# First block with the bias turned earlier and 512-column products; last block with another product order, prior sums on GpSimd, a seed that takes its prior, and outputs in pieces

## The chip, the core and the metric

The kernel runs on one core of one Trainium2 chip. The metric is the time of one execution in microseconds on the device. Three runs of the kernel before took 848.92, 849.00 and 849.01 us; the median is 849.0 us.

## What is computed

x has 16 x 512 = 8192 rows of 768 columns, w1 is 768 x 3072, w2 is 3072 x 768, all in float32:

```python
def reference(x, w1, b1, w2):
    y = np.matmul(x, w1) + b1
    y = np.maximum(y, 0)
    return np.matmul(y, w2).astype(np.float32)
```

## The kernel before

**Blocks.** The 8192 rows are cut into 8 blocks of 1024 rows, and the 3072 hidden columns into two chunks. This gives 16 iterations (`NIT`): eight blocks for the first chunk, then eight for the second. In each one the first matrix product makes a piece y of the hidden layer (1024 rows by 1536 columns, in float16), and the second multiplies it by the matching 1536 rows of w2. What the first chunk gives is stored to the output; what the second chunk gives is added to it in DRAM, by stores on GpSimd's queue that accumulate. The last iteration (`final`) is an exception: seven of its eight output tiles (`LAST_DIRECT`) are not accumulated in DRAM. What the first chunk left there, the *prior*, is loaded into the tile x by SP's queue (line 1174), added on the core, and the finished tile is stored by SP's queue.

**Fewer products.** Both products are done by a bilinear scheme, as Strassen's is one: sums and differences of blocks of x, of w1, of y and of w2 are formed first (`X_SUMS`, `W1_SUMS`, `Y_SUMS`, `W2_SUMS`; on DVE, lines 828, 844, 1046, 862), and then 20 block products for each half of the hidden chunk take the place of 24, and 26 in the second matrix product take the place of 32. A product of the second kind is 6 matmuls of 128 x 128 by 384 columns (line 1199): two row tiles, j = 0 and 1, of three each. The products are gathered in *chains*: a chain keeps one pair of PSUM banks, and between its products it hands over what it has so far by operations (`SECOND_OPS`, line 1210 on ACT, line 1216 on DVE): a "sum" is kept in SBUF for another chain, a "seed" is written into the PSUM banks in which another chain starts, and an "out" finishes an output tile. `SECOND_ORDER` and, in the last iteration, `LAST_ORDER` say in which order the 26 products run.

**The first block** has no such sums: its products are plain (`add_plain`, line 983), because the sums of w1 are not there yet. A plain product makes 128 hidden columns (strip, j) for 512 rows (half m of the block). It runs in two parts of 256 rows (`parts` = 2, twelve matmuls) or at once (`parts` = 1, six matmuls of 512 columns). The x of this block is turned on PE (`add_transpose_first`, line 925): row tiles s = 0 to 3 of the first half in float32, loaded by the queues of SP and ACT in turn (line 711), then four of the second half in float16, loaded by GpSimd's queue. Each turn is two PSUM banks, copied to x by DVE and ACT (lines 933 and 931). The bias (`add_bias`) is loaded by ACT's queue (line 679), turned on PE (line 945), and made into small tables by DVE (lines 948 to 963). ACT takes each plain product out of PSUM with bias and relu (line 992).

**Order.** Nothing is scheduled on the chip. `Graph` plans the whole program when it is built: each piece of work is a task with an engine, a cost in ns, and what it reads and writes; `Graph.run` places tasks on five engines by these costs and due times, with PE's tasks kept in the order in which they were added; then the instructions are emitted in the order of planned starts, and each engine runs its own in that order, waiting on semaphores. So a changed cost or an added task can reorder work on DVE, ACT, GpSimd and SP near it.

**The end.** In the last iteration an "out" on DVE adds the prior to what is in PSUM. If another chain's sum belongs to it as well, that is added to the prior first (`prior_task`, line 1260, on DVE at a planned cost of 955 ns, or on GpSimd at 1850 if the operation is listed in `LAST_POOL`, which is empty before). `LAST_FOLD` = (5,) adds the prior of operation 5 into PSUM ahead of its chain's last product (`fold`, line 1277). The last "out", operation 1 (output tile 3, after product 20), is taken out in two halves by DVE (`half`), stored by the queues of ACT and SP (`store_half`, line 1245).

**The guard.** ACT also sums squares of the inputs (lines 767, 876, 890); a flag says at the end whether they were in the range for which float16 does, and a general path stands behind a branch that this data does not take.

Of the kernel before, what the change touches and what calls it, by code (L numbers as in the profile page):

```python
# [124 lines left out]
    24, 5, 20)  # L125
LAST_ORDER = (13, 15, 4, 17, 10, 8, 12, 18, 3, 0, 1, 14, 2, 19, 21, 11, 25, 23, 7, 16, 5, 6, 22,
    9, 24, 20)
LAST_FOLD = (5,)
LAST_DIRECT = (0, 1, 2, 3, 4, 5, 7)
LAST_POOL = ()  # L130

# [455 lines left out]
class Fast:  # L587
# [120 lines left out]
    def prologue(self):  # L708
        nc = self.nc
        for s in range(4):  # L710
            (nc.sync, nc.scalar)[s % 2].dma_start(out=self.s[:, s],
                                                  in_=self.xf[s * P:(s + 1) * P, :])
# [12 lines left out]
        for _ in range(8):  # L725
            nc.tensor.matmul(self.ps[:, 7, 0:P], lhsT=self.ones, rhs=self.ones, start=True,
                             stop=True)

    def presets(self):
        g = self.g  # L730
# [447 lines left out]
    def add_second(self, it):  # L1178
        c = it // self.NSB
        nc = self.nc  # L1180
        final = it == self.NIT - 1
# [10 lines left out]
        def pair(reg):  # L1192
            a = reg.at[0]
            return self.ps[:, a:a + 2, 0:NH]

        def product(p, ch, start):
            for j, h in ((j, h) for j in range(2) for h in range(3)):
                m0 = h * QM + j * P
# [37 lines left out]

        def half(t, j, dest):
            ch, a, _, _, _, to, _ = SECOND_OPS[t]
            out = self.s[:, dest.at[0], 0:NH]
            combine(nc.scalar if t in folds and j == 0 else nc.vector, out, pair(bank[ch])[:, j],  # L1240
                    a, None if t in folds else self.prior(to)[:, j], 1)

        def store_half(to, j, dest):
            s = self.s[:, dest.at[0], 0:NH]
            (nc.scalar, nc.sync)[j].dma_start(out=self.rows_of(it, to)[:, j], in_=s)

# [35 lines left out]
        where = {p: ch for ch, chain in enumerate(SECOND_CHAINS) for k, p in chain if k == "m"}  # L1282
        folds = set()
        for kind, n in steps:
            if kind == "m":
# [40 lines left out]
            else:  # L1326
# [4 lines left out]
                else:  # L1331
                    dest = bank[to] = Reg("ps", 2, seeded=1, leaves=1)
            if what == "out" and final and n == last:
                for j in range(2):
                    dest = Reg("s")
                    e = "ACT" if n in folds and j == 0 else "DVE"
                    self.g.add(e, 500, lambda t=n, j=j, dest=dest: half(t, j, dest),
                               reads=reads, writes=[dest])
                    self.g.add(("ACT", "SP")[j], 100, lambda to=to, j=j, dest=dest: store_half(to, j, dest),
                               reads=[dest], writes=[("half", j)], lat=3.5, dma=0.6)  # L1340
                continue
# [5 lines left out]
            if what == "out":  # L1347
# [3 lines left out]
                           reads=[dest], writes=[("out", self.block(it), to)],  # L1351
                           lat=3.5 if direct else 9.0, dma=1.2 if plain else 2.45)

# [191 lines left out]
```

## Time and profile before

| | |
|---|---|
| median of three runs (848.92 to 849.01) | 849.0 us |
| the profiled execution: span from its first to its last instruction | 847.4 us |
| PE busy | 839.4 us (99%) |
| DVE busy | 737.9 us (87%) |
| ACT busy | 569.4 us (67%) |
| GpSimd (POOL) busy | 164.1 us (19%) |
| granted clock of PE, mean | 0.999 |

The profiled execution has no time beside its span; the runs' median is 1.6 us above it.

A row of a timeline has the start, the length, the engine, the line, the operation, its tile written and read, its shape, the number of instructions merged in the row, and in brackets how long the engine sat idle ahead of it and what ended that. PEld is PE's weight load, which overlaps its products; a "q" behind an engine's name is its queue of DMA issues. PE's products overlap each other: the length of one (326 ns for 384 columns) is longer than the distance to the next.

### The profile page before, as it was taken

To read this page: it belongs to the slowest core of one execution; us is meant where nothing else is said; L and a number is where in the kernel's file an instruction comes from. 1 tells how busy PE (TensorE), PEld (TensorE's weight loads), DVE (VectorE), ACT (ScalarE), POOL (GpSimd) and SP (SyncE) were. 2 spreads that over 40 slices of the span, in tenths; PEclk is the share of its full clock that TensorE was granted. 3 is DMA by queue.
4 is the path that set the end of the run, shared out by engine and by line. 5 is a ranking of instruction groups with operands and counts; after the bars stand their busy time and mean duration, and the time that the engine had idled before them with its cause. 6 is when DMAs were issued, how large, how long until landed. Compare 5 with 4: busy or idle time off the path is not lost. (4 is left out here: it accounts for less than half of the span.)

```text
span 847.4 us, 16784 instructions
## 1 busy us (share of the span) xinstructions
PE 839.4 (99%) x6381; PEld 625.5 (74%) x6381; DVE 737.9 (87%) x1231; ACT 569.4 (67%) x1203; POOL 164.1 (19%) x179
## 2 busy tenths in 40 slices
PE   8999999999999999999999999999999999999997
PEld 7558778686786867768687686877868678686874
DVE  5898987969889697998999979798896979979788
ACT  5866876778677695756858558766757666456463
POOL 5210011102111010010030503224041230501300
PEclk9999999999999999999999999999999999999999
DMA  9996497978988678594793977979789797985836
GB/s 213 202 180 176 81 233 105 163 183 133 222 113 148 169 126 192 95 223 150 224 187 65 192 123 124 187 106 178 125 128 150 116 173 113 147 134 75 146 117 169
DMA packets 170967, 128.93 MB, mean 152 GB/s; under 512 B 93804, under 2 KB 169348, under 8 KB 170884
## 3 DMA queue, kind: packets, MB, share of 16 engines
q0 software_dynamic: 56560, 68.82, 53.1%
q1 hardware_dynamic: 113856, 58.02, 28.3%
q8 instruction: 50, 0.82, 0.4%
q10 hardware_dynamic: 468, 1.00, 0.3%
q14 instruction: 33, 0.27, 0.1%
HBM read 73.54 MB, written 69.21 MB: 168 GB/s over the span
## 5 line engine op out<-in xcount | busy, mean ns | idle before, releaser
L1199 PE MATMUL ps<-v,y 128*128 128x384 f16 x2496 | 408.4, 326 | 0.0
L1073 PE MATMUL ps<-x,v 128*128 128x256 f16 x3600 | 395.7, 273 | 0.0
L1073 PEld LDWEIGHTS <-v 128*128 128x128 f16 x3600 | 352.2, 98 | 42.4 <-issue 0.2
L1199 PEld LDWEIGHTS <-y 128*128 128x128 f16 x2496 | 244.2, 98 | 160.0 <-issue 0.2
L1210 ACT ACTIVATE s<-ps 128x384 f32<-128x384 f32 (+1 forms) x244 | 153.0, 646 | 121.3 <-PE ps L1199 120.2
L1046 DVE TENSOR_TENSOR y<-y 128x768 f16<-128x768 f16 (+1 forms) x384 | 219.4, 619 | 2.6
L1116 DVE CUSTOM_DVE_ANT_0 y<-ps,s 128x512 f16<-128x512 f32 x240 | 156.0, 686 | 54.4 <-ACT s L1113 41.4
L1252 POOL DMA_DIRECT2D out_dram<-s x78 | 93.9, 1470 | 145.4 <-ACT s L1210 97.0
L1113 ACT ACTIVATE s<-ps,bt 128x256 f32<-128x256 f32 x180 | 75.3, 470 | 62.5 <-PE ps L1073 56.7
L828 DVE TENSOR_TENSOR x<-x 128x768 f16<-128x768 f16 (+1 forms) x210 | 113.7, 579 | 1.3
L1113 ACT ACTIVATE y<-ps,bt 128x256 f16<-128x256 f32 x180 | 69.5, 486 | 10.8 <-PE ps L1073 10.8
L1210 ACT ACTIVATE ps<-ps 128x384 f32<-128x384 f32 (+1 forms) x144 | 67.9, 509 | 8.1 <-PE ps L1199 6.6
L1216 DVE TENSOR_TENSOR s<-ps,s 128x768 f32<-128x768 f32 x74 | 70.5, 953 | 1.2 <-issue 0.3
L706 POOL DMA_DIRECT2D xn<-in_x_dram x30 | 25.9, 863 | 214.0 <-DMA x<-xn 99.5
L1216 DVE TENSOR_TENSOR s<-s,ps 128x768 f32<-128x768 f32 x60 | 57.1, 951 | 2.2 <-DVE s L1216 0.5
L767 ACT ACTIVATE junk<-xn 128x768 f16<-128x768 f16 x64 | 54.0, 843 | 0.3
L1255 POOL DMA_DIRECT2D out_dram<-s x15 | 17.7, 1181 | 169.5 <-ACT s L1210 157.7
L1113 ACT ACTIVATE ps<-ps,bt 128x256 f32<-128x256 f32 x60 | 26.7, 445 | 32.4 <-PE ps L1073 31.4
L1109 ACT ACTIVATE ps<-ps 128x512 f32<-128x512 f32 x60 | 35.3, 588 | 4.1 <-DVE y L1116 3.5
L1124 DVE TENSOR_TENSOR s<-s,ps 128x512 f32<-128x512 f32 x30 | 20.6, 688 | 17.7 <-PE ps L1073 17.7
L983 PE MATMUL ps<-x,v 128*128 128x256 f16 (+1 forms) x216 | 32.0, 308 | 0.7 <-DVE x L933 0.7
L1119 DVE SCALAR_TENSOR_TENSOR s<-ps,bt,s 128x256 f32<-128x256 f32 x60 | 26.1, 477 | 4.4 <-PE ps L1073 4.4
(60 smaller groups left out, 304.8 us busy)
## 6 DMA issues: line engine op xcount, KB each, us to landing
out_dram<-s POOLq DMA_DIRECT2D x93, 384.0 KB, 8.8
out_dram<-s SPq DMA_DIRECT2D x70, 384.0 KB, 6.6
xn<-in_x_dram POOLq DMA_DIRECT2D x28, 768.0 KB, 9.7
x<-out_dram SPq DMA_DIRECT2D x7, 384.0 KB, 3.5
v<-in_w_dram POOLq DMA_DIRECT2D x6, 384.0 KB, 10.6
v<-in_w_dram POOLq DMA_DIRECT2D x12, 192.0 KB, 9.1
w1d<-in_w_dram POOLq DMA_DIRECT2D x6, 384.0 KB, 6.5
w2d<-in_w_dram POOLq DMA_DIRECT2D x12, 192.0 KB, 4.9
```

The source lines that it names most:

```text
L767: self.nc.scalar.activation(out=self.junk, in_=self.xn[:, s, :], func=ACTF.Square, accum_out=self.stat[:, self.stat_at["x"] + i:][:, 0:1])
L828: self.nc.vector.tensor_tensor(out=self.two(x, out), in0=self.two(x, in0), in1=self.two(x, in1), op=ALU.add if sign > 0 else ALU.subtract)
L983: nc.tensor.matmul(self.ps[:, ps.at[0], cols], lhsT=self.v1[:, gi, 2 * h + k2, k, j * P:(j + 1) * P], rhs=rhs, start=(k2 == 0 and k == 0), ...
L1046: self.nc.vector.tensor_tensor(out=self.two(self.y, out), in0=self.two(self.y, in0), in1=self.two(self.y, in1), op=ALU.add if sign > 0 els ...
L1073: nc.tensor.matmul(self.ps[:, at, j * self.QM:(j + 1) * self.QM], lhsT=self.v1[:, gi, self.w1s[c][gi][FIRST_V[p]], k, j * P:(j + 1) * P], ...
L1109: nc.scalar.activation(out=out, in_=ps, scale=float(a), func=func if kind == "out" else ACTF.Copy)
L1113: nc.scalar.activation(out=out[:, j], in_=ps[:, j], func=func, scale=float(a), bias=beta(j))
L1116: nc.vector._custom_dve(TENSOR_ADD_SAT, out=out, in0=ps, in1=s, s0=F_MAX, s1=0.0)
L1199: nc.tensor.matmul(self.ps[:, bank[ch].at[j], 0:NH], lhsT=self.y[:, ys[SECOND_U[p]], m0:m0 + P], rhs=self.v2[:, slot[SECOND_V[p]], h, :], ...
L1210: nc.scalar.activation(out=out, in_=ps, func=ACTF.Copy, scale=float(a))
L1216: engine.tensor_tensor(out=out, in0=in0, in1=in1, op=ALU.add if a == b else ALU.subtract)
L1252: nc.gpsimd.dma_start(out=rows, in_=out, accum_op=ALU.add)
```

## The change

Four things at the start. The bias is loaded between ACT's two loads of x and is turned on PE between the turns of row tiles 1 and 2 (before: between the two parts of the first product). Nine of the twelve plain products of strips 0 to 2 run at once with 512 columns; the first one of the first half and the first two of the second half stay in two parts. Row tiles 0 and 1 of the second half are turned ahead of a whole product (before: between its parts), and after row tiles 2 and 3 the product of strip 0, j = 1 runs between the two parts of that of j = 0. ACT takes all plain products of strips 0 to 2 out of PSUM in one operation. In the last iteration the order of products becomes ..., 23, 25, 7, 16, 5, 6, 9, 22, 20, 24, so operation 0 (output tile 2, after product 24) is the last. Nothing is folded. Operation 10, which writes the seed of product 24's bank, is done by DVE in two halves, and takes the prior of output tile 2 with it (`LAST_TAKE`), so the bank holds the finished sum after product 24. That product is added in two halves, each with its own wait. Operation 0 then only copies: 384 columns of j = 0 on ACT, stored by SP; 192 columns of j = 1 on DVE, stored by SP; the other 192 on ACT, stored by ACT (`LAST_PARTS`). Operation 1 (output tile 3) goes out in two halves on DVE, both stored by SP (`LAST_HALVES`). The sums of priors for operations 1, 3, 4 and 5 move to GpSimd (`LAST_POOL`).

```diff
+LAST_ORDER = (13, 15, 4, 17, 10, 8, 12, 18, 3, 0, 1, 14, 2, 19, 21, 11, 23, 25, 7, 16, 5, 6, 9,
+    22, 20, 24)
+LAST_FOLD = ()
+LAST_TAKE = {10: 0}
+LAST_HALVES = (1,)
+LAST_PARTS = ((0, 0, 384, "ACT", "SP"), (1, 0, 192, "DVE", "SP"), (1, 192, 384, "ACT", "ACT"))
 LAST_DIRECT = (0, 1, 2, 3, 4, 5, 7)
-LAST_POOL = ()
+LAST_POOL = (1, 3, 4, 5)
...
                                                   in_=self.xf[s * P:(s + 1) * P, :])
-        self.load_bias()
+            if s == 1:
+                self.load_bias()
...
-        g.preset("b1_rows", 5.0)
+        g.preset("b1_rows", 6.0)
...
         for s in range(4):
             self.add_transpose_first(0, s)
+            if s == 1:
+                self.add_bias()
         plain = self.add_plain
+
+        def turns(*tiles):
+            for s in tiles:
+                self.add_transpose_first(1, s)
         for strip in range(3):
             for j in range(2):
-                between = None
-                if strip == 0 and j == 0:
-                    between = self.add_bias
-                elif strip == 2 and j == 1:
-                    between = lambda: [self.add_transpose_first(1, s) for s in (0, 1)]
-                plain(strip, j, 0, 2, 2 if strip == 1 else 1, between)
-        plain(0, 0, 1, 2, 1, lambda: [self.add_transpose_first(1, s) for s in (2, 3)])
-        plain(0, 1, 1, 2, 1)
+                if strip == 2 and j == 1:
+                    turns(0, 1)
+                plain(strip, j, 0, 2 if strip == 0 and j == 0 else 1, 1)
+        plain(0, 0, 1, 2, 1, lambda: [turns(2, 3), plain(0, 1, 1, 2, 1)])
         for strip in (1, 2):
             for j in range(2):
-                plain(strip, j, 1, 2, 2 if strip == 1 else 1)
+                plain(strip, j, 1, 1, 1)
...
+        def part(t, j, cols, dest, e):
+            ch, a = SECOND_OPS[t][:2]
+            combine(nc.scalar if e == "ACT" else nc.vector, self.s[:, dest.at[0], cols],
+                    pair(bank[ch])[:, j, cols], a, None, None)
+
+        def store_part(to, j, cols, dest, e):
+            (nc.scalar if e == "ACT" else nc.sync).dma_start(
+                out=self.rows_of(it, to)[:, j, cols], in_=self.s[:, dest.at[0], cols])
...
+                if final and t == last and SECOND_CHAINS[ch][-2] == ("m", n):
+                    for j in range(2):
+                        self.g.add("PE", 488, lambda p=n, ch=ch, start=start, j=j:
+                                   product(p, ch, start, (j,)),
+                                   reads=self.y_keys(u) + [("w2", w, h) for h in range(3)] +
+                                   ([] if start else [bank[ch]]) +
+                                   ([("taken", t, j)] if t in taken_by else []),
+                                   writes=[("last", j)] + ([] if t in taken_by else [bank[ch]]))
+                    continue
...
+                for j, c0, c1, e, q in LAST_PARTS:
+                    dest = Reg("s")
+                    cols = slice(c0, c1)
+                    self.g.add(e, 100 + 1.05 * (c1 - c0),
+                               lambda t=n, j=j, cols=cols, dest=dest, e=e:
+                               part(t, j, cols, dest, e),
+                               reads=[("last", j)] + (reads if j else []), writes=[dest])
+                    self.g.add(q, 100, lambda to=to, j=j, cols=cols, dest=dest, q=q:
+                               store_part(to, j, cols, dest, q),
+                               reads=[dest], writes=[("part", j, c0)], lat=3.5, dma=0.545 * (c1 - c0) / 384)
+                continue
+            taken = LAST_TAKE.get(n) if final else None
+            if taken is not None:
+                assert engine == "ACT" and what == "seed" and SECOND_OPS[taken][1] == 1
+                folds.add(taken)
+                prior_task(taken)
+                of = SECOND_OPS[taken][5]
                 for j in range(2):
+                    self.g.add("DVE", 548, lambda ch=ch, a=a, of=of, dest=dest, j=j: combine(
+                        nc.vector, pair(dest)[:, j], pair(bank[ch])[:, j], a,
+                        self.prior(of)[:, j], 1),
+                        reads=reads + self.prior_keys(of) + ([dest] if j else []),
+                        writes=[("taken", taken, j)] + ([] if j else [dest]))
+                continue
...
```

More of the change, by code (lines that the diff above doesn't have):

```diff
@@ L125 @@
     24, 5, 20)
-LAST_ORDER = (13, 15, 4, 17, 10, 8, 12, 18, 3, 0, 1, 14, 2, 19, 21, 11, 25, 23, 7, 16, 5, 6, 22,
-    9, 24, 20)
-LAST_FOLD = (5,)
+LAST_ORDER = (13, 15, 4, 17, 10, 8, 12, 18, 3, 0, 1, 14, 2, 19, 21, 11, 23, 25, 7, 16, 5, 6, 9,
[4 more added lines that the diff above has]
+LAST_PARTS = ((0, 0, 384, "ACT", "SP"), (1, 0, 192, "DVE", "SP"), (1, 192, 384, "ACT", "ACT"))
 LAST_DIRECT = (0, 1, 2, 3, 4, 5, 7)
-LAST_POOL = ()
+LAST_POOL = (1, 3, 4, 5)
 X_FUSE = (3,)
@@ L1194, in pair, with product @@
             return self.ps[:, a:a + 2, 0:NH]
-        def product(p, ch, start):
-            for j, h in ((j, h) for j in range(2) for h in range(3)):
+        def product(p, ch, start, rows=(0, 1)):
+            for j, h in ((j, h) for j in rows for h in range(3)):
                 m0 = h * QM + j * P
@@ L1235, in operation @@
                         None if alone else sum_of(kept[u]), b)
[L1237 to L1245, printed above, removed]
+        def part(t, j, cols, dest, e):
[5 more added lines that the diff above has]
+                out=self.rows_of(it, to)[:, j, cols], in_=self.s[:, dest.at[0], cols])
         def store(to, reg, plain):
@@ L1283, in add_second @@
         folds = set()
+        taken_by = set(LAST_TAKE.values()) if final else ()
         for kind, n in steps:
@@ L1333, in add_second @@
             if what == "out" and final and n == last:
+                assert n in folds
+                for j, c0, c1, e, q in LAST_PARTS:
[8 more added lines that the diff above has]
+                               reads=[dest], writes=[("part", j, c0)], lat=3.5, dma=0.545 * (c1 - c0) / 384)
@@ new lines, in add_second @@
+                continue
[5 more added lines that the diff above has]
+                of = SECOND_OPS[taken][5]
+                for j in range(2):
+                    self.g.add("DVE", 548, lambda ch=ch, a=a, of=of, dest=dest, j=j: combine(
[4 more added lines that the diff above has]
+                continue
@@ L1334, in add_second @@
+            if what == "out" and direct and n in LAST_HALVES:
+                assert n not in folds
                 for j in range(2):
                     dest = Reg("s")
[L1336 to L1340, printed above, removed]
+                    self.g.add("DVE", 548, lambda j=j, to=to, ch=ch, a=a, dest=dest: combine(
+                        nc.vector, self.s[:, dest.at[0], 0:NH], pair(bank[ch])[:, j], a,
+                        self.prior(to)[:, j], 1), reads=reads, writes=[dest])
+                    self.g.add("SP", 100, lambda to=to, j=j, dest=dest: store_part(
+                        to, j, slice(0, NH), dest, "SP"),
+                        reads=[dest], writes=[("half", to, j)], lat=3.5, dma=0.545)
@@ L1351, in add_second @@
                            reads=[dest], writes=[("out", self.block(it), to)],
-                           lat=3.5 if direct else 9.0, dma=1.2 if plain else 2.45)
+                           lat=3.5 if direct else 9.0,
+                           dma=1.09 if direct else 1.2 if plain else 2.45)
     def add_check(self):
```

## The prediction

> **What bounds the kernel now.** I read the page first, then the busy time by stretches, then the timelines of the first 21 us and the last 32 us, engine by engine. The page and the stretches say that one engine sets the time:
>
> ```profile
> span 847.4 us, 16784 instructions
> PE 839.4 (99%) x6381; PEld 625.5 (74%) x6381; DVE 737.9 (87%) x1231; ACT 569.4 (67%) x1203; POOL 164.1 (19%) x179
> ...
> 20.00:60.00 40.00, 39.79 (x243) 1.00 1.11 188
> 60.00:800.00 740.00, 740.00 (x5688) 1.00 0.82 149
> ```
>
> In the stretches (start and end, length, PE busy us and instructions, clock, DMA) PE has no idle time from 20.2 us on, at a granted clock of 1.00, and the rows of the last block below go on without one. So what is taken from PE ahead of 20 us, and what lies between its last product and the end of the span, count in full, as long as no other engine falls behind in between. Here is the start, PE alone:
>
> ```profile
> 5.55 1.50 PE L925 MATMUL ps<-ident,s 128*128 128x128 f32 x12 [0.48 <-DMA s<-in_x_dram]
> 7.64 1.50 PE L925 MATMUL ps<-ident,s 128*128 128x128 f32 x12 [0.58 <-DMA s<-in_x_dram]
> 9.46 0.82 PE L983 MATMUL ps<-x,v 128*128 128x256 f16 x6 [0.32 <-DVE x L933]
> 10.21 0.24 PE L945 MATMUL ps<-ident,b_rows 24*128 24x24 f32 x1
> 10.38 6.72 PE L983 MATMUL ps<-x,v 128*128 128x256 f16 x60
> 16.93 0.83 PE L925 MATMUL ps<-ident,xn 128*128 128x128 f16 x12
> 17.61 1.59 PE L983 MATMUL ps<-x,v 128*128 128x256 f16 x12
> 19.03 0.83 PE L925 MATMUL ps<-ident,xn 128*128 128x128 f16 x12
> 20.21 1.03 PE L983 MATMUL ps<-x,v 128*128 128x256 f16 x8 [0.35 <-DVE x L933]
> ```
>
> The end, on PE:
>
> ```profile
> 816.78 25.66 PE L1199 MATMUL ps<-v,y 128*128 128x384 f16 x156
> ```
>
> on DVE:
>
> ```profile
> 840.03 1.82 DVE L1260 TENSOR_TENSOR x<-x,s 128x768 f32<-128x768 f32 x2
> 841.77 1.88 DVE L1216 TENSOR_TENSOR s<-ps,x 128x768 f32<-128x768 f32 x3
> ```
>
> and on SP's queue, with the time to landing of this line's stores:
>
> ```profile
> 843.68 0.34 SPq L1245 DMA_DIRECT2D out_dram<-s  x1
> ...
> DMA to landing us min/median/max: 2.5/2.6/2.6
> ```
>
> The last product ends at 816.78 + 25.66 = 842.44, DVE's last half at 841.77 + 1.88 = 843.65, the last store is issued at 843.68, and the span ends 847.4 - 843.7 = 3.7 us later, of which 2.6 are that store's way to its landing. So 1.24 us lie between the last product and the last store's issue, and the rest is a fixed tail.
>
> **The change, part by part: the start.** *Bias.* Its turn (line 945) moves from between two halves of the first product to between the turns of row tiles 1 and 2. A 256-column product costs (6.72 - 0.27) / 59 = 0.109 us to the next one (60 of them in 6.72, the last one's own 0.27 taken off). Six from 9.46 end their issue at 10.11, but the next one starts at 10.38: **0.27** goes. In its new place it stands in PE's wait for x rows: the first turns are over at 5.55 + 1.50 = 7.05, the next cannot start before 7.64, and it takes 0.24. The step carries its DMA along: ACT's queue now issues the bias between its two loads of x, so the second is issued later by the bias issue:
>
> ```profile
> 0.97 0.87 ACTq L711 DMA_DIRECT2D s<-in_x_dram  x2
> 1.87 0.65 ACTq L679 DMA_DIRECT2D b_rows<-in_b_dram  x1
> ...
> DMA to landing us min/median/max: 4.3/5.1/6.1
> ```
>
> That row tile (3) is needed half-way through the second turns, at 7.64 + 0.75 = 8.4. With its issue at 1.4 + 0.65 = 2.05 and the longest way of 6.1 it lands at 8.15, so nothing is lost; from the shortest way, 6.4. The bias itself, issued at 1.4, lands by 7.5 at the very worst, when PE would be waiting anyway. What follows it on DVE does queue ahead of copies of x:
>
> ```profile
> 6.11 1.21 DVE L933 CAST x<-ps 128x384 f16<-128x384 f32 x2 [4.87 <-PE ps L925]
> 8.19 1.21 DVE L933 CAST x<-ps 128x384 f16<-128x384 f32 x2 [0.87 <-PE ps L925]
> 10.48 0.18 DVE L948 COPY b1y<-ps 128x24 f32<-128x24 f32 x1 [1.07 <-PE ps L945]
> ...
> 11.49 0.17 DVE L959 TENSOR_SCALAR bt<-b1y 128x8 f32<-128x8 f32 x1
> ```
>
> Eight small operations (10.48 to 11.49, 1.0 us) now stand before the third copy, and two more (0.3) before the fourth. They start when DVE's second copy is done (6.11 + 1.21 = 7.32), so the third copy starts at 8.3 in place of 8.19 and the fourth ends near 8.3 + 0.56 + 0.3 + 0.56 = 9.7 in place of 9.40. The product that needs them is the second half, at 10.11: hidden, with 0.4 us to spare.
>
> *Turns of x.* From 17.61 twelve products take 12 x 0.109 = 1.31, so PE is free at 18.92 but goes on at 19.03 (0.11); twelve turns take 17.61 - 16.93 = 0.68, so it is free at 19.71 and goes on at 20.21 (0.50). Both waits are for copies of the x just turned. In the changed order a full product (1.30) or a half product of another strip (0.66) stands between a turn and its first reader; the reader used to come 20.21 - 19.03 = 1.18 after the turns began, and now 0.68 + 0.66 = 1.34 after. **0.61** goes, 0.16 to spare.
>
> *512 columns.* Nine of twelve blocks go from twelve 256-column products (12 x 0.109 = 1.31) to six of 512:
>
> ```profile
> 30.65 12.03 PE L983 MATMUL ps<-x,v 128*128 128x512 f16 x55
> ```
>
> (12.03 - 0.38) / 54 = 0.216, six are 1.295. **0.13** for nine blocks; the columns cost what they cost. Start: 0.27 + 0.61 + 0.13 = **1.01 us**. The first product itself still waits for its weights at 9.46.
>
> **The end.** *Waits inside the last block.* The page has this line for all 16 blocks:
>
> ```profile
> L1199 PE MATMUL ps<-v,y 128*128 128x384 f16 x2496 | 408.4, 326 | 0.0
> ```
>
> 408.4 / 16 = 25.52 us for a block of 156, six of which (one product of the order) take 0.98; the last block takes 25.66. Its last wait is for the seed that ACT writes, with one product as cover:
>
> ```profile
> 839.49 0.80 ACT L1210 ACTIVATE ps<-ps 128x768 f32<-128x768 f32 x1 [3.42 <-PE ps L1199]
> ```
>
> The change swaps two pairs of products and lets DVE write that seed in two halves, each with the prior in it, while a product stands between and the reader is split in halves too: DVE has 0.98 us for the first (0.55) and 1.46 for both (1.01). **0.14** goes.
>
> *After the last product.* Before, DVE does 0.95 + 0.55 + 0.55 behind the last two products. Now the prior is in PSUM before the last product starts; half of its result is copied while the other half is multiplied. What is left is a copy of 192 columns on DVE: 0.55 for 384 columns, 0.95 for 768, so 0.001 us a column and 0.35. ACT's 192 columns stand behind it: in the built order ACT waits for DVE's copy, so its store comes at about +0.75, with SP's. SP is what comes last: four stores (two halves of one output, one half and 192 columns of the other) follow each other. Two issues back to back take 0.88 (the x loads above), 0.44 each. The second of the four is ready with DVE's last sum, about where PE ends; two more issues follow it, so the last is issued 0.88 after the last product, in place of 1.24: **0.36**. The landing I leave as it is: the 384 KB stores of line 1250 ahead of it took
>
> ```profile
> DMA to landing us min/median/max: 2.4/2.5/2.8
> ```
>
> and the 192 KB ones 2.5 to 2.6, so size hardly shows.
>
> *Sums on GpSimd.* Four of six sums of priors go from DVE (0.95 each) to GpSimd, the operation of line 1277 goes, and ACT loses two operations of 0.8. DVE's last five operations above follow each other without a gap, so this is what lets DVE take the seed. The trace has no such sum on GpSimd; the nearest rows:
>
> ```profile
> L660 POOL CAST ident<-ident 128x128 f16<-128x128 f32 x1 | 0.3, 291 | 0.1
> ...
> L672 POOL MEMSET high<- 128x24 f32 x2 | 0.2, 108 | 0.0
> ```
>
> 0.29 - 0.10 for 128 columns of one input is 1.5 ns a column, 1.25 us for 768; two inputs read one after the other, 2.4. I take 1.85, the middle. GpSimd's last store is
>
> ```profile
> 830.32 1.18 POOL L1252 DMA_DIRECT2D out_dram<-s  x1 [4.59 <-DVE y L1046]
> ```
>
> One sum stands ahead of it, in the 4.59 us that GpSimd waits there now, so the store is not held up. Three stand in a row behind it, from 831.50, or 830.5 with the start's 1.0 off: they end at 830.5 + 3 x 1.85 = 836.05. The last one is read by the output of product 6, the fifth from the end, which ends at 841.28 - 4 x 0.975 = 837.4. Covered by 1.3 us, so up to 2.3 us a sum costs nothing. [...]
>
> **Sum:** 1.01 + 0.14 + 0.36 = 1.51 us off a span of 847.4, so 845.9. The runs' median is 849.0, 1.6 above the span, and I let that stand: **847.5**.
>
> **Rivals.** *The tail shortens too.* Smaller last stores, four close together, and the 1.1 us behind the landing: if the last store lands 0.4 sooner (2.2), 847.1. For it: its 192 columns are a quarter of the smallest full output. Against it: 192 KB and 384 KB land alike. If four queued stores delay each other, the same 0.4 the other way, 847.9.
>
> *GpSimd is slow.* At 2.4 us a sum the three end at 837.7, 0.3 late; DVE then does two outputs and the seed (2 x 0.87 + 2 x 0.47 = 2.7) and is done at 840.4 where product 24 wants 840.3 with a half: about 0.4 lost, 847.9.
>
> *GpSimd and DVE's sums of y block each other.* The first GpSimd sum falls among these:
>
> ```profile
> 824.87 1.54 DVE L1046 TENSOR_TENSOR y<-y 128x768 f16<-128x768 f16 x2
> ...
> 829.99 0.95 DVE L1260 TENSOR_TENSOR x<-x,s 128x768 f32<-128x768 f32 x1
> ```
>
> If a sum of y has to wait for all of it, DVE is 1.85 late, gets 0.95 back where line 1260 no longer runs at 829.99, and PE loses up to 0.9 for want of y: 848.4. [...]
>
> *All of DVE blocks, and it is slower than before.* From 830.5 to product 24 at 840.3 DVE has eight operations of 0.87 (two in a row take 1.82) and two halves of 0.47, 7.9 us, and GpSimd 5.55. Taken in turn that is 13.45 in 9.8: 3.6 us late, less 1.5, gives 851.1. It decides once DVE operations that read PSUM cannot run beside a GpSimd sum. Against it: at 829.99 DVE's sum takes its 0.95 beside the store that GpSimd works on from 830.32.
>
> *The start is given back* where DVE has no gap (sums of w2 and y, 30 to 60 us): 848.5. Against it: PE never waits there now.
>
> **How the numbers follow.** Forecast 0.50, shorter tail 0.24, slow GpSimd or queued stores 0.08, blocked sums of y 0.06, start given back 0.04, all blocked 0.08. What this kernel's measurement can tell from no change is about 0.2%, 1.7 us, so faster means below 847.3. The forecast (give or take 0.3) has a quarter of its 0.50 there: 0.24 + 0.13 = 0.37 faster; 0.09 slower; 0.54 within. Range: from the short tail with a little luck at the start, 846.9, to the blocked sums, 848.6.
>
> **What would show it.** Bias at about 7 us on PE; products from 9.46 to 21 us with no wait for DVE; last product near 841.3; no PE wait in the last block; GpSimd sums of 1.25 to 2.3 us with DVE at 0.95 beside them; last SP store issued 0.9 after PE's end. Wrong if PE ends later than 841.6, or the span ends less than 4.3 or more than 5.0 after it.

## The result, and the profile after

The changed kernel takes 852.18 us (five runs, 851.83 to 853.05), the kernel before 849.01 (848.92 to 849.03). The ratio is 1.0041 with a 95% interval of 1.0030 to 1.0051: slower by 3.2 us, where 1.5 us less was forecast. The profiled execution took 851.83 us with a span of 850.2, against 847.4. Its page:

```profile
span 850.2 us, 16682 instructions
PE 839.7 (99%) x6327; PEld 619.9 (73%) x6327; DVE 738.3 (87%) x1229; ACT 567.7 (67%) x1199; POOL 172.6 (20%) x183
```

PE is as busy as before (839.7 against 839.4 us), so the 2.8 us of span are time in which it does nothing. They lie in three places. The first is the start; the timeline of PE:

```profile
7.04 0.89 PE L929 MATMUL ps<-ident,s 128*128 128x128 f32 x6
8.26 0.87 PE L929 MATMUL ps<-ident,s 128*128 128x128 f32 x6 [0.33 <-DMA s<-in_x_dram]
10.23 6.65 PE L987 MATMUL ps<-x,v 128*128 128x256 f16 x36 [1.09 <-DVE x L937]
16.71 0.83 PE L929 MATMUL ps<-ident,xn 128*128 128x128 f16 x12
```

and of DVE:

```profile
7.37 0.51 DVE L963 TENSOR_SCALAR bt<-b1y 128x8 f32<-128x8 f32 x2
...
8.00 0.70 DVE L963 TENSOR_SCALAR bt<-b1y 128x8 f32<-128x8 f32 x3
8.74 0.17 DVE L967 TENSOR_TENSOR bt<-bt,b1y 128x8 f32<-128x8 f32 x1
8.82 0.56 DVE L937 CAST x<-ps 128x384 f16<-128x384 f32 x1
9.29 0.21 DVE L963 TENSOR_SCALAR bt<-b1y 128x8 f32<-128x8 f32 x1
...
9.63 0.55 DVE L937 CAST x<-ps 128x384 f16<-128x384 f32 x1
```

PE waits once more for x, at 8.26, and the first product starts at 10.23 instead of 9.46: it waits for DVE's copies, the last of which ends at 9.63 + 0.55 = 10.18, behind the small tables. From there to the last block the kernel makes up 0.87 us (806.45 instead of 807.32) of the 1.01 forecast, with no gap at the turns. The second place is the last block, on PE:

```profile
816.68 12.84 PE L1205 MATMUL ps<-v,y 128*128 128x384 f16 x78
829.68 1.15 PE L1205 MATMUL ps<-v,y 128*128 128x384 f16 x6 [0.17 <-DVE y L1052]
831.01 7.97 PE L1205 MATMUL ps<-v,y 128*128 128x384 f16 x48 [0.18 <-DVE y L1052]
839.28 4.28 PE L1205 MATMUL ps<-v,y 128*128 128x384 f16 x24 [0.29 <-DVE s L1222]
```

It lasts from 816.68 to 843.56, 26.88 us, where 25.52 was forecast. (The brackets give less than the loss, since a row ends with its last matmul's whole 0.33 us, and the next usually starts 0.16 us after it began.) DVE and GpSimd at the same time:

```profile
824.77 3.52 DVE L1052 TENSOR_TENSOR y<-y 128x768 f16<-128x768 f16 x2
825.26 2.21 POOL L1265 TENSOR_TENSOR x<-x,s 128x768 f32<-128x768 f32 x1
...
833.32 6.72 POOL L1265 TENSOR_TENSOR x<-x,s 128x768 f32<-128x768 f32 x3 [1.96 <-DVE s L1222]
...
835.18 0.96 DVE L1222 TENSOR_TENSOR s<-ps,x 128x768 f32<-128x768 f32 x1 [0.22 <-PE ps L1205]
836.06 2.31 DVE L1265 TENSOR_TENSOR x<-x,s 128x768 f32<-128x768 f32 x1
```

Beside GpSimd's sums two sums of y take 3.52 us (1.54 before), a sum of priors 2.31 instead of 0.95; DVE's operation that reads PSUM keeps its 0.96 though GpSimd is at its sums. The durations of GpSimd's four (min/median/max ns):

```profile
L1265 POOL TENSOR_TENSOR x<-x,s x4: 1798/2332/2533, 825.3 to 837.5; 128x768 f32<-128x768 f32 x4
```

The third place is the landing of the last stores (line 1249, five stores):

```profile
L1249 SPq DMA_DIRECT2D out_dram<-s x4: 345/402/428, 843.4 to 844.8; - x4
...
DMA to landing us min/median/max: 2.2/4.1/4.3
```

The first two land after 2.2 and 2.5, the other three after 4.1 to 4.3. On the DMA engines the one thing that is new there is an instruction fetch, one packet of 16384 bytes on queue 8. (That the instructions are PE's is taken from where it goes when the length of PE's stream is changed: 839.7 us in e3, 839.3 in e6 (845.3 in e5), 844.0 in e12, all below.) In the view of DMA queues (packets, MB, share) it lies, before, in the stretch from 837 to 838 us:

```profile
q8 instruction: 1, 0.02, 7.7%
```

and after, in the stretch from 845.5 to 846.5, among the packets of the last stores:

```profile
q1 hardware_dynamic: 197, 0.24, 68.9%
q10 hardware_dynamic: 131, 0.09, 29.3%
q8 instruction: 1, 0.02, 5.9%
```

The sum of what differs from the forecast's 845.9: last block begun at 816.68 and not 0.9 sooner, +0.9; waits in the block +1.36; last store issued 1.24 and not 0.88 behind PE's end, +0.36; landing 4.1 and not 2.6, +1.5; from landing to the end 1.3 and not 1.1, +0.2. That is 4.3, and 845.9 + 4.3 = 850.2. (In the 25.52 every matmul counts 0.16 us, the distance to the next; a row ends with the last matmul's whole 0.33. So 0.14 of the 1.36 is no wait: the kernel before has 25.66 in one unbroken row.)

### The profile page after: what moved, and what is told of

The parts are those of the page before. It is cut to its first block, busy times and chain, and to the rows that moved or that the text cites. A ratio compares the mean times of both kernels' runs of the same rounds, so it can differ in the third digit from the quotient of the medians.

```text
span 850.2 us, 16682 instructions
## 1 busy us (share of the span) xinstructions
PE 839.7 (99%) x6327; PEld 619.9 (73%) x6327; DVE 738.3 (87%) x1229; ACT 567.7 (67%) x1199; POOL 172.6 (20%) x183
## 5 line engine op out<-in xcount | busy, mean ns | idle before, releaser
L1216 ACT ACTIVATE s<-ps 128x384 f32<-128x384 f32 (+2 forms) x245 | 153.0, 643 | 126.9 <-PE ps L1205 125.5
L987 PE MATMUL ps<-x,v 128*128 128x512 f16 (+1 forms) x162 | 31.6, 355 | 1.1 <-DVE x L937 1.1
L848 DVE TENSOR_TENSOR v<-v 128x768 f16<-128x768 f16 x48 | 24.8, 554 | 6.4 <-DMA v<-in_w_dram 5.9
```

Source lines behind the costliest of these rows:

```text
L987: nc.tensor.matmul(self.ps[:, ps.at[0], cols], lhsT=self.v1[:, gi, 2 * h + k2, k, j * P:(j + 1) * P], rhs=rhs, start=(k2 == 0 and k == 0), ...
L1216: nc.scalar.activation(out=out, in_=ps, func=ACTF.Copy, scale=float(a))
```

## The experiments

A number of a run is the median of its timed runs; the kernel before, run beside them on the same chip, took 849.05 to 849.33.

**Three suspects, each undone, and all together.** The bias load behind all loads of x; nothing on GpSimd; PE's stream padded to its old length.

```diff
# e1
-            if s == 1:
-                self.load_bias()
+        self.load_bias()
# e2
-LAST_POOL = (1, 3, 4, 5)
+LAST_POOL = ()
# e3
-        for _ in range(8):
-            nc.tensor.matmul(self.ps[:, 7, 0:P], lhsT=self.ones, rhs=self.ones, ...)
+        for _ in range(70):
+            nc.tensor.matmul(self.ps[:, 7, 0:P], lhsT=ones16, rhs=ones16, ...)
```

Expected of e1:

> The changed kernel with the bias load behind all four loads of x again, as before the change. Theory (the bias load on ACT's queue holds back row tile 3, which lands at 8.22 instead of 7.16 us, and the strip of w1 behind it, 9.91 instead of 9.28): row tile 3 lands near 7.2, the first product starts at 9.5 instead of 10.23, and the time falls by 0.77 us, to 851.4 from 852.18. Rival (the turns of x or the strip set that start, whatever the order of the loads): the first product stays near 10.2 and the time near 852.2.

Expected of e2:

> The changed kernel with the four sums of the last block on VectorE again (nothing on GpSimd there). Theory (GpSimd's sums hold up the VectorE sums that have both inputs in SBUF): the y sum of 2.94 us takes 0.95 again, the sum of 2.31 us takes 0.95, and PE's waits at 829.19 and 830.50 are gone; but VectorE then has four sums of 0.95 us more to do and is late near the end, where 0.4 to 0.8 us of PE wait come back, and its last piece comes 1.3 us or more behind PE's end. Time 851.5 to 852.2. Rival (the long y sum is long for another reason): it stays near 2.9 us and the waits stay.

Expected of e3:

> The changed kernel with PE's 8 float32 warm-up products at the start replaced by 70 products of float16 at 128 columns (3.9 us, in PE's idle head), so that PE's stream is as long as before the change. Theory (the instruction fetch of 16384 bytes lies at a fixed count of PE instructions, and the 108 instructions saved moved it from 837.4 to 845.9 us, onto the last stores): the fetch is back near 837, the last stores land 2.6 us after their issue instead of 4.1 to 4.3, and the time falls by 1.5 us, to 850.7. Rival (the stores in pieces of 192 columns, or four of them at once, land late by themselves): the landing stays above 4 us and the time near 852.2.

Expected of e4:

> All three edits together: the bias load behind the loads of x, the four sums on VectorE, PE's stream as long as before the change. By the theories: -0.77, -0.3 (between 0 and -0.7) and -1.5 from 852.18, near 849.6. By the rivals the time stays above 851.

e1 took 852.93 us and refuted its theory. All loads of x came in time again, yet in the timeline of PE:

```profile
7.80 0.21 PE L948 MATMUL ps<-ident,b_rows 24*128 24x24 f32 x1 [0.65 <-DMA b_rows<-in_b_dram]
7.94 1.55 PE L928 MATMUL ps<-ident,s 128*128 128x128 f32 x12
11.07 6.65 PE L986 MATMUL ps<-x,v 128*128 128x256 f16 x36 [1.57 <-DVE x L936]
```

PE now waits for the late bias, and the first product waits longer, for DVE: so more than the landing is at work, and DVE's queue became the new suspect. e2 took 853.54. In its timeline of DVE the sums of y are short again:

```profile
826.07 1.54 DVE L1052 TENSOR_TENSOR y<-y 128x768 f16<-128x768 f16 x2
```

but two waits came near 838 and 843 us, the stores piled up behind DVE, and the start of the profiled execution was slow for a reason taken up below. e3 took 851.22 (expected 850.7): the fetch lies near 840, and its last five stores land after (min/median/max)

```profile
DMA to landing us min/median/max: 2.2/2.4/2.5
```

so the gain at the end is there, though the 70 products took 5.6 us and not 3.9 and put the turns off by a microsecond. e4 took 852.18 where 849.6 was expected: the edits inherit e1's and e2's new waits and e3's late turns. A sum of three repairs is no repair while each is not clean.

**The bias undone as a whole, and the 512 columns undone on top of it.**

```diff
# both: load_bias() behind the loads of x, and
-            if s == 1:
-                self.add_bias()
...
-                plain(strip, j, 0, 2 if strip == 0 and j == 0 else 1, 1)
+                plain(strip, j, 0, 2 if strip == 0 and j == 0 else 1, 1,
+                      self.add_bias if strip == 0 and j == 0 else None)
# e6 besides: parts = 2 for all twelve plain products
```

Expected of e5:

> The changed kernel with the whole edit of the bias undone: its load behind the four loads of x, its turn on PE between the two halves of the first product, as before. Theory (the bias turn waits for the bias, and the nine tables that VectorE makes from it stand in VectorE's queue ahead of its copies of row tiles 2 and 3; that, not the landing alone, sets the first product): the first product starts near 9.5 us instead of 10.23, PE pays 0.2 for the bias turn, the time falls by 0.5 to 0.6 us, to 851.6; the last stores still land more than 4 us after their issue. Rival (the turns of x and the copies are late whatever the bias does): first product above 10, time near 852.2.

Expected of e6:

> As the run with the bias edit undone, and the nine products of 512 columns as two of 256 columns again, which gives PE's stream its 108 instructions back; the turns of x and the last block stay changed. Theory (the fetch of PE's instructions is moved by their count): the fetch of 16384 bytes lies near 838 us, the last stores land 2.2 to 2.6 us after their issue, and the time is 1.5 us less than with 512 columns, near 850.1. Rival (the fetch is only a bystander): landing above 4 us, time 851.7.

e5 took 851.48, and its first product started at 9.51. e6 took 850.05. The landings of their last five stores, e5 (fetch between 845 and 846.5 us):

```profile
DMA to landing us min/median/max: 2.2/4.0/4.3
```

e6 (fetch between 839 and 840.5):

```profile
DMA to landing us min/median/max: 2.2/2.3/2.5
```

The same five stores in the same pieces land 1.7 to 1.8 us sooner (median and slowest) when nine products have more and shorter instructions 800 us earlier. So the bias edit cost 0.7 us, the 512 columns 1.4, and the pieces do no harm.

**Two parts of the change alone on the kernel before:** the turns (e7, all products at 256 columns) and the last block (e8).

Expected of e7:

> The kernel before with one part of the change alone: the turns of x of the second half at their new places in the first block (all products at 256 columns in two parts; bias and last block as before). Theory (that part does what was predicted): the waits of 0.12 and 0.26 us at 18.2 and 19.6 us and the gaps around the turns are gone, 0.5 to 0.6 us less, near 848.45. Rival (the gain is given back in the first block): 849.0.

Expected of e8:

> The kernel before with the change of the last block alone (its order, the four sums on GpSimd, the outputs in pieces); the first block as before. Theory (GpSimd's sums hold up VectorE's sums with two inputs in SBUF, and the pieces do no harm by themselves): PE waits about 1.4 us in the last block, the last store is issued 1.2 us after PE's end, lands 2.6 us later since the fetch stays near 838, and the time is 850.2 (849.9 to 850.6). Rival (the pieces land late by themselves): landing above 4 us, time 851.8. Rival (GpSimd's sums cost nothing once the first block is as before): 848.5.

e8 took 850.36, with PE's waits at the same places as in the changed kernel and landings of 2.2 to 2.5. e7 took 849.78, but its ten runs fell in two groups, four at 848.52 to 848.66 and six at 849.72 to 850.29. The profiled one is of the second; the duration of its turns (min/median/max ns):

```profile
L925 PE MATMUL ps<-ident,s x20: 421/421/446, 5.9 to 9.9; 128*128 128x128 f32 x20
```

Of the runs of the kernel before beside it, 5 of 28 lay at 850.34 to 850.75 too. So PE's pace at the start may be what parts the two groups; that is tested next.

**The load without the tables, PE without a gap, two sums on GpSimd, and 512 columns alone.**

```diff
# e9, on the changed kernel: early load kept, add_bias between the parts of the first product
# e10, on e7
-        for _ in range(8):
+        for _ in range(10):
# e11, on e8
-LAST_POOL = (1, 3, 4, 5)
+LAST_POOL = (3, 4)
# e12, on the kernel before
-                plain(strip, j, 0, 2, 2 if strip == 1 else 1, between)
+                plain(strip, j, 0, 2 if between else 1, 1, between)
...
-                plain(strip, j, 1, 2, 2 if strip == 1 else 1)
+                plain(strip, j, 1, 1, 1)
```

Expected of e9:

> The changed kernel with the bias load early, as changed (between ACT's two loads of x), but the bias turn and so VectorE's tables between the two halves of the first product, as before. It parts the load from the tables. Theory A (the tables ahead of the copies of row tiles 2 and 3 cost most): row tile 3 lands at 7.8 to 8.2 us, its turns end near 9.1, its copy is done near 9.7, and the first product starts as soon as that or the strip of w1 is there, at 9.6 to 9.95 instead of 10.23; time near 851.6. Theory B (the landing of row tile 3 and of the strip costs all): first product at 10.1 to 10.3, time 852.0 to 852.4.

Expected of e10:

> The kernel before with the new places of the turns alone, and ten warm-up products on PE instead of eight, so that PE has no idle gap before the first turn of x. The runs with the turns alone lay in two groups, 848.52 to 848.66 and 849.72 to 850.29, and the profiled one of the second group had its turns of x at 213 ns each instead of 109 up to 10.1 us. Theory (PE was left at half rate because its activity broke off between 5.1 and 5.8 us): with ten the turns run at 109 ns in all or nearly all runs, median 848.6 (848.4 to 848.9), so it beats the kernel before. Rival (the half rate comes and goes whatever PE does there): two groups again, median between 848.6 and 850.2.

Expected of e11:

> The kernel before with the change of the last block alone, but two of the four sums (3 and 4) on GpSimd instead of four (1, 3, 4, 5); sums 1 and 5 on VectorE. Theory (what costs is a GpSimd sum at the same time as a VectorE sum with both inputs in SBUF): the waits at 829 and 830.6 us (0.68 together) are gone, one of up to 0.8 us is left near 837, the last store is issued about 1 us earlier than at 844.86, and the time is 849.3 against 850.36 with four. Rival (the order of the last block costs it, not GpSimd): the time stays near 850.3.

Expected of e12:

> The kernel before with eight of the products of the first block at 512 columns alone (96 PE instructions fewer); turns, bias and last block as before. Theory (the fetch of PE's instructions moves to about 845 us; before's last stores are issued at 842.7 to 843.7 and most of their packets are done by then, so it costs them little, up to 0.6): 849.0, between 848.8 and 849.6. Rival (any kernel with the shorter stream loses the 1.6 us of late landing): 850.4.

e9's first product in the timeline of PE:

```profile
9.65 0.83 PE L987 MATMUL ps<-x,v 128*128 128x256 f16 x6 [0.77 <-DMA v<-in_w_dram]
```

With the early load and without the tables in the way it starts 0.58 us sooner and waits for the weights, not for DVE: theory A. (The time, 851.9, was 0.3 above the expected; the profiled execution has another wait of 0.6 in the bracket, near 418 us, behind an ACT operation that waits for a load of w2. e1 has one of 0.9 there.)

e10 took 848.73, all ten runs at 848.57 to 849.01, one group, with turns of

```profile
L925 PE MATMUL ps<-ident,s x24: 272/273/303, 5.8 to 9.2; 128*128 128x128 f32 x24
```

e11 took 850.69, hardly other than e8, against an expected 849.3 (its lower group lies at 850.0 to 850.19). The waits at 829 and 830.6 are gone, but sums 1 and 5 are back on DVE and collide with the two that are left:

```profile
L1262 DVE TENSOR_TENSOR x<-x,s x4: 951/1320/1702, 833.0 to 838.1; 128x768 f32<-128x768 f32 x4
L1262 POOL TENSOR_TENSOR x<-x,s x2: 2493/2502/2512, 834.0 to 836.5; 128x768 f32<-128x768 f32 x2
```

(again min/median/max ns) and on PE one longer wait takes the place of e8's three:

```profile
838.82 6.11 PE L1202 MATMUL ps<-v,y 128*128 128x384 f16 x36 [0.85 <-ACT ps L1213]
```

e12 took 850.97: the 512 columns alone make the kernel before slower by 1.8 us. My expectation was wrong in the direction that matters: with the fetch at 844 us the last two stores (line 1245) landed after

```profile
DMA to landing us min/median/max: 4.4/4.5/4.5
```

though they were issued at 843.6 and 844.0. With the late fetch these two whole halves land later too (2.5 and 2.6 in the kernel before, whose fetch is at 837), as the five pieces do.

**The last block taken apart, the warm-up alone, and the bias in a place where PE waits.**

```diff
# e13, on e8
-LAST_POOL = (1, 3, 4, 5)
+LAST_POOL = ()
# e14, on the kernel before
-LAST_POOL = ()
+LAST_POOL = (1, 3, 4, 5)
# e15, on the kernel before: ten warm-up products for eight
# e16, on e10
             self.add_transpose_first(0, s)
+        self.add_bias()
         plain = self.add_plain
```

Expected of e13:

> The kernel before with the change of the last block alone, and all four sums on VectorE (none on GpSimd). Theory A (the new order has no room for the four sums anywhere: on VectorE they make it late, on GpSimd they hold VectorE up): no wait for the y sum, but waits of 0.8 to 1.0 us near 837 and 842, the last store issued 2 us or more behind PE's end, and the time at 850.0 to 851, no better than 850.36 with four on GpSimd. Theory B (GpSimd's sums alone cost the 1.3 us): without them 849.0.

Expected of e14:

> The kernel before with one constant changed: the four sums 1, 3, 4 and 5 of the last block on GpSimd, the old order and all else kept. Theory A (GpSimd's sums hold up VectorE's sums with two inputs in SBUF in any order): the y sum beside the first of them takes 2.5 to 3 us instead of 0.95, PE waits 1 to 2 us in the last block, and the time is 850.0 to 851.2. Theory B (it is the new order that costs, the sums on GpSimd relieve VectorE): 848.7 to 849.0.

Expected of e15:

> The kernel before with ten warm-up products on PE instead of eight and nothing else. Theory (the runs of the kernel before that lie at 850.3 to 850.7 are those whose turns of x ran at half rate): one group of runs at 848.9 to 849.3, none above 850. Rival: two groups as before.

Expected of e16:

> The version with the turns at their new places and ten warm-up products, and the bias turn behind the fourth turn of x, where PE waits 0.6 us for VectorE's copy anyway; VectorE's tables come behind its four copies of x. Theory (the bias edit failed by the place of its tables and its early load, and the 0.2 us of the turn between the halves of the first product can be had): the first product starts no later than in the version without (9.76), has no gap of 0.2 us after its sixth matmul, and the time is 848.5, 0.2 less than 848.73. Rival (nothing to gain there): 848.7 or more.

e13 took 851.6: the new last block is slowest without GpSimd. PE ends at 842.18 + 1.14 = 843.32, DVE only at 844.65, and SP's stores pile up behind it, the last issued at 845.9:

```profile
842.18 1.14 PE L1202 MATMUL ps<-v,y 128*128 128x384 f16 x6 [0.33 <-DVE ps L1219]
...
844.30 0.35 DVE L1215 TENSOR_SCALAR s<-ps 128x192 f32<-128x192 f32 x1
```

The last stores of e13, issues (min/median/max ns, first and last start) and landings:

```profile
L1246 SPq DMA_DIRECT2D out_dram<-s x4: 433/454/825, 844.0 to 845.9; - x4
...
DMA to landing us min/median/max: 2.6/2.9/3.7
```

e14 took 850.76: GpSimd's four sums in the old order cost 1.4 us against 849.33 beside it. Its y sums are as long as in the changed kernel (two in 3.52 us), and PE waits for them at 830.26 and 831.60. Later DVE waits for the second of GpSimd's last three sums, and with it ACT's seed and PE; a row of DVE's timeline:

```profile
838.98 0.95 DVE L1216 TENSOR_TENSOR s<-x,ps 128x768 f32<-128x768 f32 x1 [1.70 <-POOL x L1260]
```

So neither the new last block nor GpSimd is the sole cause. Each costs by itself (e13 2.3 more than the kernel before beside it, e14 1.4), and together they cost 1.3 (e8): with the old order the sums on GpSimd lose 1.4, with the new one they win 1.0. What in the new last block costs the 2.3, the order or the seed that takes its prior, no run parts.

e15 took 849.08, all runs at 848.86 to 849.63, while 9 of 31 runs of the kernel before lay at 850.31 to 850.75. So the two warm-up products remove the slow starts. Between e15 and e10, which ran on another chip, lie the 0.35 us of the turns. The rows of e10 from its first product to the product behind the second turns:

```profile
9.76 0.81 PE L983 MATMUL ps<-x,v 128*128 128x256 f16 x6 [0.32 <-DVE x L933]
...
19.88 1.36 PE L983 MATMUL ps<-x,v 128*128 128x256 f16 x11
```

That is 10.12 us, against 20.21 - 9.46 = 10.75 before: 0.63 is gone there. About 0.15 of it is lost again on the way: from 19.88 to the last block at 816.60 e10 takes 796.72 us, the kernel before 816.78 - 20.21 = 796.57.

e16 took **848.12** (848.10 to 848.48), ratio 0.9986 with an interval of 0.9976 to 0.9995: faster than both kernels, the only one here whose interval says so; it is 0.96 below e15, which ran beside it with the same warm-up. Rows of the timelines of PE and, below the dots, of DVE (its third and fourth copy):

```profile
9.15 0.24 PE L945 MATMUL ps<-ident,b_rows 24*128 24x24 f32 x1
9.41 6.72 PE L983 MATMUL ps<-x,v 128*128 128x256 f16 x60
...
8.28 1.21 DVE L933 CAST x<-ps 128x384 f16<-128x384 f32 x2 [0.89 <-PE ps L925]
```

The bias turn fills PE's wait, the tables follow the copies, and 60 matmuls run without the gap of 0.27. And the first product starts at 9.41, ahead of the end of the fourth copy at 9.49, for which the first product of the kernel before, of the changed one and of e10 waits. The built programs say why: its PSUM bank used to be the one that this copy empties, and with the bias turn ahead of it the first product gets another. That was not foreseen; it is part of why e16 gained 0.6 on e10 and not 0.2 (how much is not separated from the loads' own scatter: e16's first turns start at 5.62, e10's at 5.85).

## Why the prediction was wrong

- **Turns of x, 0.61: right, in part given back.** The gaps are gone (after: 16.71, then on without a wait), and the start of e10 is 0.63 shorter; as a time of the kernel they gave 0.35 to 0.4, since about 0.15 is lost again before the last block. So the rival "the start is given back" holds for that small part, though not at 30 to 60 us: at 493.9 two matmuls of e10 stand 0.30 us apart in place of 0.11 (in e7 and the changed kernel at the same place), and why stays open.
- **Bias, 0.27: this step failed, and with its sign.** The prediction put the tables ahead of DVE's copies and found 0.4 us to spare, with the third copy at 8.3 and the fourth ending at 9.7. Measured: 8.82 and 10.18. The small operations were costed by the 1.0 us that eight take in their old place; here they took longer (two 0.51, three 0.70), from 7.15 to 8.8; why, no run here parts. It also bounded row tile 3 by the longest way of 6.1 from an issue at 2.05 (8.15); the turn that waits for it starts at 8.26, and PE stood ready from 7.04 + 0.89 = 7.93, since the other turns had come sooner: there was no margin. And it took only the product's second half, at 10.11, to need the fourth copy, as a reader of x; but its first matmul starts in the bank that this copy empties, and waits for it. The prediction put that wait down to the weights, though its own row at 9.46 names DVE's copy. e9 and e5 show it: with the tables out of the way the first product starts at 9.65 and 9.51. The whole edit cost 0.7 (e5); in the right place it pays (e16).
- **512 columns, 0.13: this step failed by what it left out.** The term counted PE's time and not that 108 instructions (54 matmuls and 54 weight loads) leave PE's stream. With them an instruction fetch moved by 8.5 us (from 837.4 to 845.9), onto the last stores: 1.4 us (e5 against e6), 1.8 on the kernel before (e12).
- **Landing left at 2.6: failed for the same reason,** not through the pieces. "Size hardly shows" holds: e8's pieces land in 2.2 to 2.5. Neither half of the rival on the tail explains the changed kernel; in e13, where SP's stores pile up, landings reach 3.7; that they delay each other there is an estimate.
- **Waits in the last block, 0.14, and sums on GpSimd at 1.85, "covered by 1.3 us": this step failed.** The shortest sum takes 1.80, as assumed; that was not what mattered. The cover was reckoned for GpSimd's own lateness and not for what it does to DVE: two y sums 3.52 for 1.54, a sum of priors 2.31 for 0.95. The rival that names this had 0.06, with one place and 0.9 us; there were two places, and 1.22 of waits. The 0.14 on top was never there to be had: PE's last block before has no wait, and the prediction compared a row that ends with a whole matmul (25.66) with a mean that counts distances (25.52). That the new last block costs 2.3 even without GpSimd (e13) was in no term.
- **All of DVE blocks, 0.08: refuted as a mechanism,** though its 851.1 lies nearest the result. DVE operations that read PSUM took 0.94 to 0.96 beside GpSimd's sums (rows of the changed kernel from 834.02 to 840.09); what took longer beside them has both inputs in SBUF, the sums of y (3.52 for 1.54) and of priors (2.31 for 0.95). The rival that blocks the sums of y had a row for its place in the trace, and deserved more than 6 chances in 100.
- **Last store 0.88 behind PE: failed by 0.36,** through DVE, which was late with all that preceded: its last copy, at 843.67, is followed by the last issue at 844.80.

## What to carry to other kernels

Count the instructions that an edit adds or removes on an engine with a long unrolled stream, and look where the next instruction fetch then falls: here 108 fewer on PE put it on the last stores, and the slowest of them landed after 4.3 us instead of 2.6. Before a sum moves to GpSimd, see what DVE does beside it: here, where that had two inputs in SBUF, both got slower (2.5 us for 1.80 and 1.70 for 0.95), and it paid only where DVE would have lost more by keeping the sums, in the new last block (851.6 in e13, 850.36 in e8). And when small work moves up, ask what it now stands ahead of on every queue that it touches: here the place that paid was the one where the engine waited anyway.

## What the hardware showed that was not expected

**Instruction fetches and stores.** With the fetch between 837 and 840 us the last stores landed within 2.6 us (before, e3, e6, e8); with it starting between 844 and 846 us the last ones took 4 to 4.5 (after, e5, e12). PE did not wait for that fetch: its last block before is one row without a gap, over the fetch at 837. How one packet of about 1 us delays three landings, the view of DMA queues shows in part. After, from 847 to 848 us (q1 and q10 are the queues of the stores, q14 brings other instructions in packets of 8192 bytes):

```profile
q1 hardware_dynamic: 7, 0.01, 4.4%
q14 instruction: 1, 0.01, 2.8%
q10 hardware_dynamic: 7, 0.01, 2.1%
```

Up to 846.5 the stores and the fetch keep all 16 DMA engines busy (68.9, 29.3 and 5.9%); here their last packets take 6.5% of them, which is one engine's worth, and they go on until 848.3. In e3 and e6, whose last store is issued at 845.8, a microsecond later than here, all five land within 2.5 us. The 6.5% fit one engine that finishes later than the others, with the stores landing when it does; that, and that it is the engine that took the fetch, is an estimate from these numbers and not shown, since a packet's engine is not in the trace. A late fetch may not be the only way: e13, which has as many PE instructions as e8 (whose fetch is at 838.3), shows landings of up to 3.7.

**Half pace at the start.** In some executions PE's turns ran 421 ns long (273 otherwise) until 10 us or later (e7; e2, whose first twelve turns took 2.79 us in place of 1.50). In e7 that cost about 1.4 us: its first product starts at 11.14, that of e10 at 9.76. The view of stretches gave PE's granted clock as 1.00 there all the same (e7, 5 to 10 us). The trace's own record of the clock begins only at 5.54 us in the kernel before and at 4.83 in the changed one; the matmuls of the warm-up, which start ahead of it, have a median of 421 ns (sixteen in 3.78 us in the kernel before), and the turns behind it 273 (twelve in 1.50). So the view's 1.00 says nothing of the time before. Ten warm-up products instead of eight removed the slow start: all thirty runs of e10, e15 and e16 lie between 848.10 and 849.63. In e10 and e16 the ten keep PE at work until 5.54 and 5.79 us, where eight end at 5.07. In e15's profiled execution they ended at 5.14, and the idle gap of 0.51 ahead of the first turn was no shorter than before (0.48); so that the gap is the cause is not shown.

**Both sides pay in a collision.** A GpSimd sum of 768 float32 took 1.80 us in the changed kernel where it began first, at 835.7 (DVE's sum, begun at 836.06, took 2.31 instead of 0.95), and 2.5 in e11 beside DVE sums, which took 1.70. The times fit the one waiting until the other is done: in e11 GpSimd's last sum ends at 839.00, and the DVE sum that began at 838.13 ends 0.82 behind it, at 839.82.
